# Loads, parameters and stores change queues in a batch-norm-and-ReLU kernel

## Chip, cores and metric

One core of one Trainium2 chip. The metric is device time in microseconds (us). The kernel before takes 83.91 us (median of 5 runs, 83.83 to 84.08). Its runs agree within 0.3%, so half a microsecond is a real difference here.

## The reference

```python
batch, channels, h, w = 32, 128, 32, 32        # x: 16.78 MB of float32
normalized = (x - running_mean[None,:,None,None]) / np.sqrt(running_var[None,:,None,None] + eps)
scaled = normalized * gamma[None,:,None,None] + beta[None,:,None,None]
return np.maximum(scaled, 0).astype(np.float32)
```

Each channel has one scale and one bias, so the kernel reads 16.78 MB, applies one activation `relu(scale*x + bias)`, and writes 16.78 MB.

## The kernel before

The 4096 rows of 1024 numbers (batch and channel together) are laid on 128 partitions, 16 consecutive rows to a partition, in two halves `t`. A half is cut into pieces by rows. Six loads (1, 1, 2, 4, 4 and 4 MiB) go out on the sync queue; four tiny parameter loads and all stores go out on the scalar queue, which is ScalarE's own.

```python
PIECES = (((0, 2), (2, 4), (4, 8), (8, 16)), ((0, 8), (8, 16)))
STORE_CUTS = {(0, 1)}
...
for t in range(T):
    for a, b in PIECES[t]:
        xt = data.tile([P, b - a, HW], F32, name=f"x{t}_{a}")
        nc.sync.dma_start(out=xt, in_=xr[t, :, a:b, :])
        tiles.append((t, a, b, xt))
raw = params.tile([Q, 4, J], F32, name="raw")
for k, src in enumerate((running_var, gamma, running_mean, beta)):
    nc.scalar.dma_start(out=raw[:, k, :], in_=src.rearrange("(q j) -> q j", j=J))
...   # a matmul spreads the parameters over the partitions; sqrt, reciprocal, products
for t, a, b, xt in tiles:
    first = a
    for j in range(a, b):
        nc.scalar.activation(out=xt[:, j-a, :], in_=xt[:, j-a, :], func=ACTF.Relu,
                             bias=bias_t[:, j:j+1], scale=scale_t[:, j:j+1])
        if j + 1 == b or (t, j + 1) in STORE_CUTS:
            nc.scalar.dma_start(out=outr[t, :, first:j+1, :], in_=xt[:, first-a:j+1-a, :])
            first = j + 1
```

## Time and profile before

| | before |
|---|---|
| time, median | 83.91 us |
| span of the profiled execution | 81.9 us |
| busiest compute engine (ScalarE) | 47% |
| bytes moved | 33.56 MB |
| mean rate over the span | 410 GB/s |

The prediction works out from the profile what bounds the kernel, and shows the lines that this rests on.

### The profile page before, as it was taken

What the parts mean: (1) busy time and instruction counts of PE and PEld (TensorE: products, weight loads), DVE (VectorE), ACT (ScalarE), POOL (GpSimd) and SP (SyncE); (2) the same over time, 40 slices, a digit from 0 to 9 for tenths busy, and PEclk for the clock granted to TensorE, in tenths of its full rate; (3) what the DMA queues carried; (4) which work ended last, traced back from release to release, by engine and by line L of the source; (5) the groups of instructions that cost most, each with busy time, mean ns of one, the idle gap of its engine ahead of it and who ended that gap; (6) DMA issues with size and microseconds to landing.
All of it is one profiled execution on the core that took longest, in us unless ns stands there. A gap on an engine that the chain in (4) does not pass through costs nothing.

```text
span 81.9 us, 119 instructions
## 1 busy us (share of the span) xinstructions
PE 0.7 (1%) x2; PEld 0.5 (1%) x2; DVE 0.8 (1%) x5; ACT 38.5 (47%) x34; POOL 0.8 (1%) x6
## 2 busy tenths in 40 slices
PE   0002000000000000000000000000000000000000
PEld 0002000000000000000000000000000000000000
DVE  0000300000000000000000000000000000000000
ACT  0600377799039999199994199993000000000000
POOL 3000000000000000000000000000000000000000
DMA  2899999989899999979789798996999899799690
GB/s 32 328 425 472 408 448 448 512 352 494 370 448 416 446 418 396 500 296 600 320 380 580 304 464 384 512 512 288 480 512 400 368 512 448 320 512 496 272 512 0
DMA packets 1936, 33.56 MB, mean 410 GB/s; under 512 B 272, under 2 KB 272, under 8 KB 528
## 3 DMA queue, kind: packets, MB, share of 16 engines
q1 hardware_dynamic: 864, 16.78, 48.4%
q10 hardware_dynamic: 1072, 16.78, 47.8%
HBM read 16.78 MB, written 16.78 MB: 410 GB/s over the span
## 4 chain that ended last, share of the span: by engine, by line
DMA 56%; ACT 11%; SPq 0%; issue 0%
DMA x<-in_x_dram 56%; ACT x L96 11%; SPq L52 0%
## 5 line engine op out<-in xcount | busy, mean ns | idle before, releaser
L96 ACT ACTIVATE x<-x,bias_t,scale_t 128x1024 f32<-128x1024 f32 x32 | 37.0, 1228 | 10.3 <-DMA x<-in_x_dram 7.9
L82 ACT ACT_TABLE_LOAD x1 | 1.3, 1283 | 2.6 <-issue 2.6
L82 ACT ACTIVATE std_t<-cols,eps_t 128x16 f32<-128x16 f32 x1 | 0.3, 273 | 4.5 <-PE cols L74 4.5
L74 PE MATMUL cols<-raw,rep 8*128 8x64 f32 x2 | 0.7, 428 | 7.7 <-DMA raw<-in_beta_dram 7.7
L74 PEld LDWEIGHTS cols<-raw,rep 8*128 8x128 f32 x2 | 0.5, 304 | 7.7 <-issue 7.7
L64 POOL TENSOR_SCALAR_AFFINE_SELECT rep<-rep 8x128 f32<-8x128 f32 x1 | 0.4, 392 | 0.1
L84 DVE RECIPROCAL rstd_t<-std_t 128x16 f32<-128x16 f32 x1 | 0.3, 254 | 7.8 <-ACT std_t L82 7.8
L63 POOL MEMSET rep<- 8x128 f32 x1 | 0.2, 195 | 0.3 <-POOLq L124 0.3
L86 DVE TENSOR_TENSOR scale_t<-cols,rstd_t 128x16 f32<-128x16 f32 x1 | 0.2, 175 | 0.1
L90 DVE TENSOR_TENSOR bias_t<-cols,ms_t 128x16 f32<-128x16 f32 x1 | 0.2, 175 | 0.0
L88 DVE TENSOR_TENSOR ms_t<-cols,scale_t 128x16 f32<-128x16 f32 x1 | 0.2, 175 | 0.0
L124 POOL MEMSET const-bfloat16-1.0<- 128x1 bf16 x1 | 0.1, 106 | 0.0
L124 POOL MEMSET const-uint8-127<- 128x1 uint8 x1 | 0.1, 106 | 0.0
L124 POOL MEMSET const-float32-0.0<- 128x1 f32 x1 | 0.1, 103 | 0.3 <-issue 0.3
L124 POOL MEMSET const-float32-1.0<- 128x1 f32 x1 | 0.1, 103 | 0.0
L61 DVE MEMSET eps_t<- 128x1 f32 x1 | 0.1, 59 | 0.9 <-PEq L124 0.9
## 6 DMA issues: line engine op xcount, KB each, us to landing
x<-in_x_dram SPq DMA_DIRECT2D x3, 4096.0 KB, 38.8
out_dram<-x ACTq DMA_DIRECT2D x3, 4096.0 KB, 27.9
x<-in_x_dram SPq DMA_DIRECT2D x2, 1024.0 KB, 5.7
x<-in_x_dram SPq DMA_DIRECT2D x1, 2048.0 KB, 11.2
out_dram<-x ACTq DMA_DIRECT2D x1, 2048.0 KB
out_dram<-x ACTq DMA_DIRECT2D x2, 512.0 KB, 18.8
out_dram<-x ACTq DMA_DIRECT2D x1, 1024.0 KB
raw<-in_running_var_dram ACTq DMA_DIRECT2D x1, 0.5 KB
```

The costliest lines, as they stand in the source:

```text
L61: nc.vector.memset(eps_t, float(eps))
L63: nc.gpsimd.memset(rep, 1.0)
L64: nc.gpsimd.affine_select(out=rep, in_=rep, compare_op=mybir.AluOpType.is_equal, fill=0.0, base=0, pattern=[[0, P // Q], [-1, Q]], channel ...
L74: nc.tensor.matmul(cols.rearrange("p k j -> p (k j)"), rep.rearrange("q r s -> q (r s)"), raw.rearrange("q k j -> q (k j)"), start=True, s ...
L82: nc.scalar.activation(out=std_t, in_=cols[:, 0, :], func=ACTF.Sqrt, bias=eps_t[:, 0:1], scale=1.0)
L84: nc.vector.reciprocal(out=rstd_t, in_=std_t)
L86: nc.vector.tensor_mul(out=scale_t, in0=cols[:, 1, :], in1=rstd_t)
L88: nc.vector.tensor_mul(out=ms_t, in0=cols[:, 2, :], in1=scale_t)
L90: nc.vector.tensor_sub(out=bias_t, in0=cols[:, 3, :], in1=ms_t)
L96: nc.scalar.activation(out=xt[:, j - a, :], in_=xt[:, j - a, :], func=ACTF.Relu, bias=bias_t[:, j : j + 1], scale=scale_t[:, j : j + 1],)
L124: nc = _bacc.Bacc("TRN2", target_bir_lowering=False, num_devices=1)
```

## The change

The intent: start the activations sooner, take store issues off ScalarE's queue, and save one store. The first load stays on the sync queue and goes out alone. The scalar queue issues the parameters first, then the other five loads, with a small square root between them that pulls the table load forward. All stores go to the sync queue. The fourth and fifth tiles are stored together.

```diff
-PIECES = (((0, 2), (2, 4), (4, 8), (8, 16)), ((0, 8), (8, 16)))
+TILES = (((0, 0, 2),), ((0, 2, 4),), ((0, 4, 8),), ((0, 8, 16), (1, 0, 8)), ((1, 8, 16),))
-            nc.sync.dma_start(out=xt, in_=xr[t, :, a:b, :])          # all six loads
-        nc.scalar.dma_start(out=raw[:, k, :], ...)                   # parameters
+        nc.sync.dma_start(out=loads[0][0], in_=loads[0][1])
+        for k, src in enumerate((running_var, gamma, running_mean, beta)):
+            nc.scalar.dma_start(out=raw[:, k, :], ...)
+        for i, (dst, src) in enumerate(loads[1:]):
+            nc.scalar.dma_start(out=dst, in_=src)
+            if i == 2:
+                nc.scalar.activation(out=first_t, in_=eps_t, func=ACTF.Sqrt)
 ...
-                    nc.scalar.dma_start(out=outr[t, :, first:j+1, :], ...)
+                        nc.sync.dma_start(out=outr[t, :, a+first:j+1, :], ...)
+            if len(pieces) == 2:      # both pieces of the double tile in one store
+                nc.sync.dma_start(out=bass.AP(tensor=outr.tensor, offset=...,
+                    ap=[[J*HW, P], [pitch, 2], [HW, b-a], [1, HW]]), in_=xt)
```

More of the change, by code (lines that the diff above doesn't have):

```diff
@@ L14 @@
 J = 16
-PIECES = (((0, 2), (2, 4), (4, 8), (8, 16)), ((0, 8), (8, 16)))
-STORE_CUTS = {(0, 1)}
+TILES = (((0, 0, 2),), ((0, 2, 4),), ((0, 4, 8),), ((0, 8, 16), (1, 0, 8)), ((1, 8, 16),))
+STORE_CUTS = {(0, 0)}
 @with_exitstack
@@ L48 @@
     tiles = []
-    for t in range(T):
-        for a, b in PIECES[t]:
-            xt = data.tile([P, b - a, HW], F32, name=f"x{t}_{a}")
-            nc.sync.dma_start(out=xt, in_=xr[t, :, a:b, :])
-            tiles.append((t, a, b, xt))
+    loads = []
+    for pieces in TILES:
+        n = len(pieces)
+        rows = pieces[0][2] - pieces[0][1]
+        xt = data.tile([P, n, rows, HW], F32, name=f"x{pieces[0][0]}_{pieces[0][1]}")
+        for i, (t, a, b) in enumerate(pieces):
+            loads.append((xt[:, i], xr[t, :, a:b, :]))
+        tiles.append((pieces, xt))
     raw = params.tile([Q, 4, J], F32, name="raw")
-    for k, src in enumerate((running_var, gamma, running_mean, beta)):
-        nc.scalar.dma_start(out=raw[:, k, :], in_=src.rearrange("(q j) -> q j", j=J))
     eps_t = params.tile([P, 1], F32, name="eps_t")
     nc.vector.memset(eps_t, float(eps))
+    first_t = params.tile([P, 1], F32, name="first_t")
+    with tc.manual_schedule(engines={mybir.EngineType.Activation, mybir.EngineType.SP}):
+        nc.sync.dma_start(out=loads[0][0], in_=loads[0][1])
+        for k, src in enumerate((running_var, gamma, running_mean, beta)):
+            nc.scalar.dma_start(out=raw[:, k, :], in_=src.rearrange("(q j) -> q j", j=J))
+        for i, (dst, src) in enumerate(loads[1:]):
+            nc.scalar.dma_start(out=dst, in_=src)
+            if i == 2:
+                nc.scalar.activation(out=first_t, in_=eps_t, func=ACTF.Sqrt)
     rep = params.tile([Q, P // Q, Q], F32, name="rep")
@@ L90 @@
     nc.vector.tensor_sub(out=bias_t, in0=cols[:, 3, :], in1=ms_t)
-    with tc.manual_schedule(engines={mybir.EngineType.Activation}):
-        for t, a, b, xt in tiles:
-            first = a
-            for j in range(a, b):
-                nc.scalar.activation(
-                    out=xt[:, j - a, :],
-                    in_=xt[:, j - a, :],
-                    func=ACTF.Relu,
-                    bias=bias_t[:, j : j + 1],
-                    scale=scale_t[:, j : j + 1],
-                )
-                if j + 1 == b or (t, j + 1) in STORE_CUTS:
-                    nc.scalar.dma_start(
-                        out=outr[t, :, first : j + 1, :], in_=xt[:, first - a : j + 1 - a, :]
-                    )
-                    first = j + 1
+    with tc.manual_schedule(engines={mybir.EngineType.Activation, mybir.EngineType.SP}):
+        for pieces, xt in tiles:
+            first = 0
+            for i, (t, a, b) in enumerate(pieces):
+                for j in range(a, b):
+                    nc.scalar.activation(
+                        out=xt[:, i, j - a, :],
+                        in_=xt[:, i, j - a, :],
+                        func=ACTF.Relu,
+                        bias=bias_t[:, j : j + 1],
+                        scale=scale_t[:, j : j + 1],
+                    )
+                    if len(pieces) == 1 and (j + 1 == b or (t, j) in STORE_CUTS):
+                        nc.sync.dma_start(
+                            out=outr[t, :, a + first : j + 1, :], in_=xt[:, 0, first : j + 1 - a, :]
+                        )
+                        first = j + 1 - a
+            if len(pieces) == 2:
+                (t0, a, b), (t1, c, _) = pieces
+                pitch = ((t1 - t0) * P * J + c - a) * HW
+                nc.sync.dma_start(
+                    out=bass.AP(
+                        tensor=outr.tensor,
+                        offset=outr[t0, :, a:b, :].offset,
+                        ap=[[J * HW, P], [pitch, 2], [HW, b - a], [1, HW]],
+                    ),
+                    in_=xt,
+                )
 _INS = ['x', 'gamma', 'beta', 'running_mean', 'running_var', 'eps']
```

## The prediction

> **What bounds the kernel now.** I read the page first, then the load by stage, then the timeline with the waits, to see whether any wait reaches the end. The page:
>
> ```profile
> span 81.9 us, 119 instructions
> PE 0.7 (1%) x2; PEld 0.5 (1%) x2; DVE 0.8 (1%) x5; ACT 38.5 (47%) x34; POOL 0.8 (1%) x6
> DMA  2899999989899999979789798996999899799690
> HBM read 16.78 MB, written 16.78 MB: 410 GB/s over the span
> DMA 56%; ACT 11%; SPq 0%; issue 0%
> ```
>
> No compute engine is busy for more than 47% of the span, and the DMA row is 7 to 9 in all slices but the first and the last. 33.56 MB must pass. The chain (the last line) is no guide here: it names the wait for the last load and then eight activations, but shows nothing of the store traffic after that. So I took the rate in the stages (columns: stretch, length, busy time of each engine with its count, clock, DMA share, GB/s):
>
> ```profile
> 0.00:2.00 2.00, 0.00 (x0) 0.00 (x0) 0.06 (x1) 0.00 (x0) 0.80 (x6) 1.00 0.20 29
> 2.00:4.00 2.00, 0.00 (x0) 0.00 (x0) 0.00 (x0) 1.28 (x1) 0.00 (x0) 1.00 0.85 324
> 4.00:14.00 10.00, 0.65 (x2) 0.49 (x2) 0.78 (x4) 3.64 (x4) 0.00 (x0) 1.00 1.07 454
> 14.00:46.00 32.00, 0.00 (x0) 0.00 (x0) 0.00 (x0) 24.43 (x22) 0.00 (x0) 1.00 0.99 422
> 46.00:80.00 34.00, 0.00 (x0) 0.00 (x0) 0.00 (x0) 9.16 (x8) 0.00 (x0) 1.00 1.01 436
> 80.00:82.00 2.00, 0.00 (x0) 0.00 (x0) 0.00 (x0) 0.00 (x0) 0.00 (x0) 1.00 0.00 0
> ```
>
> From 4 us to 80 us the 16 DMA engines are full (share 0.99 to 1.07, so a little over one packet in flight each) in all stages: loads alone, loads beside stores, stores alone. 33.56 MB at the 436 GB/s of the pure store stage is 77.0 us. The span is 81.9, so only 4.9 us are not this transfer: some 2 before the first packet, about half a microsecond of slow start (324 GB/s between 2 and 4), 1.3 to 1.9 after the last packet, and around a microsecond lost between.
>
> What counts next is how much stored data is queued when the loads run out. In the stretch from 14 to 46 us the two queues moved (packets, MB, share of 16 engines):
>
> ```profile
> q1 hardware_dynamic: 384, 11.53, 83.9%
> q10 hardware_dynamic: 399, 1.96, 14.7%
> ```
>
> q1 is the load queue, q10 the store queue. They sent nearly equally many packets, but loads have 32 KB in each (eight rows per partition) and the first stores 4 KB (one row). So the stores hardly move until the loads are over at about 46 us, and pile up. The timeline says when work was handed over:
>
> ```profile
> 8.42 0.27 ACT L82 ACTIVATE std_t<-cols,eps_t 128x16 f32<-128x16 f32 x1 [4.52 <-PE cols L74]
> 9.72 1.24 ACT L96 ACTIVATE x<-x,bias_t,scale_t 128x1024 f32<-128x1024 f32 x1 [1.03 <-DVE bias_t L90]
> 23.86 9.16 ACT L96 ACTIVATE x<-x,bias_t,scale_t 128x1024 f32<-128x1024 f32 x8 [3.32 <-DMA x<-in_x_dram]
> 33.05 0.34 ACTq L104 DMA_DIRECT2D out_dram<-x  x1
> 34.81 9.16 ACT L96 ACTIVATE x<-x,bias_t,scale_t 128x1024 f32<-128x1024 f32 x8 [1.79 <-DMA x<-in_x_dram]
> 44.00 0.34 ACTq L104 DMA_DIRECT2D out_dram<-x  x1
> 46.79 9.16 ACT L96 ACTIVATE x<-x,bias_t,scale_t 128x1024 f32<-128x1024 f32 x8 [2.82 <-DMA x<-in_x_dram]
> 55.97 0.34 ACTq L104 DMA_DIRECT2D out_dram<-x  x1
> ```
>
> Four stores with 0.5+0.5+1+2 = 4 MiB (4.19 MB) precede the three large ones. By 46 us only 1.96 MB of them have gone; the rest, 2.23 MB, needs 2.23/0.436 = 5.1 us, to about 51. So the first large store, issued at 33.05, has nothing to do for 18 us, and the last, issued at 55.97, isn't reached before 51 + 2 x 4.19/0.436 = 70.5. ScalarE has some 15 us to spare at the end.
>
> **What the skill says.** The Trainium skill, "DMA: Bandwidth & Descriptors", section "Issuing engines are not separate DMA queues", says that transfers from sync and scalar run on the same 16 engines and that a second issuing engine saves only sequencer time. The trace agrees: share about 1.0 whether one queue works or two. Its section "Queues, rings and completion order" says that each engine alternates between queues packet by packet; 384 against 399 packets agrees. "Where 436 GB/s comes from" puts the ceiling of the 16 ports at 435 GB/s; the store stage shows 436, so nothing is left there for a queue arrangement. "ScalarE: Activation LUTs", "What ACT_TABLE_LOAD costs", has a load at about 1283 ns; the trace shows 1.28 us, between 2.6 and 3.9, beside idle waiting.
>
> **The change, part by part.**
>
> *First load alone on the sync queue.* It is still issued at 0.81, as the first instruction of that queue. Zero change of the start of the stream. The second load now comes from the scalar queue behind four parameter issues (0.59, 0.29, 0.31 and 0.45 us in the timeline, done at 2.53), so at 2.6 instead of 1.2. The first load's 1.05 MB needs 2.4 us at 436 GB/s, and with the slow start it drains at about 5. The second load's issue at 2.6 plus one microsecond from issue to first packets (0.81 to about 1.8 for the first) is 3.6: in time. I allow 0 to 0.4 us for an engine that changes queue[...].
>
> *Parameters.* Their tiny packets alternated with two loads' packets of q1, and the last landed at about 7.6. Now only the first load stands against them, and what is left follows when it drains: landing at about 5.5. Matmul to first main activation took 9.72 - 7.73 = 2.0 us, so the activations can start at about 7.6 instead of 9.7: 2 us earlier.
>
> *Five loads and the table load on ScalarE.* Three loads at 0.40 us median end at about 3.8, table load and the new small square root 1.6 more (5.4), two loads 0.7 (6.1). That ends before the 6.3 at which the matmul result is there. Costs nothing. The trace has eight semaphores for all transfers, reused in order of issue (in before, a load sat 4.1 us for a parameter's landing). The fifth and sixth load are ninth and tenth transfer; they would wait for the first load or the first parameter, landing by about 5.3, so the table load fills just that time.
>
> *Stores on the sync queue.* Seven issues of 0.34 to 0.38 us, 2.4 us in sum, leave ScalarE; three of them (0.42 to 0.46 us gaps) stood between activations with data present. With the earlier start ScalarE then waits for loads instead, as it already does for the fourth to sixth tile (3.3, 1.8 and 2.8 us). Nothing reaches the end. A store becomes available some 2 to 3 us sooner, so perhaps two or three more small packets per engine go between loads: loads end some 0.5 to 1 us later (at 47), and exactly as much less store traffic is left.
>
> *Merged store.* The fourth and fifth tiles leave together as 8.39 MB when the fifth is done. It landed at 34.8; I take 35.5, plus 9.2 us, so issue at about 44.7 in place of 33.05 and 44.00. The four stores ahead of it last to about 51. Slack 6 us, against some 1 us from issue to first packets. One store's completion entries saved: under 0.1 us. The packets stay 32 KB (two runs of eight rows per partition).
>
> Sum: 81.9 + 0 (start) + 0.1 (queue change, middle of 0 to 0.4, less what is saved) + 0 (rate, bytes unchanged) + 0 (tail, the last store is again queued 14 us early) = 82.0, and the unprofiled time is about what it was, 83.9.
>
> **The rivals.** (1) *The merged store runs the DMA dry.* If the early stores drained well before 44.7, engines would idle until it arrives. For it: the first of its halves is held back by 11 us. Against it: 1.96 MB in 32 us beside loads. Only a share of half the bytes for stores would empty the queue by 30; then loads alone fill the engines to about 50 anyway, and the gap would be 1 to 1.5 us: 85 to 85.5. (2) *The sooner start gains.* The intent of the change: activations 2 us earlier, no store issues on ScalarE. If ScalarE were on the path the gain would be 2 to 3 us: 81.5. The chain's 11% for ScalarE speaks for it, the full DMA row from 46 to 80 against it. (3) *A load on ScalarE's queue waits for a semaphore of a late transfer,* holding activations back. Eight semaphores and ten early transfers make it possible. Even 5 us later the store queue would still fill before the loads end: 83.9. Only a late last store (waiting for the merged one to land) would open a gap of 1.5 to 2 us: 85.7. (4) *Mixed stage runs better or worse.* At 422 instead of 436 GB/s it costs 32 x 14/436 = 1.0 us; other packet pairs might win or lose a third of that: 83.6 to 84.2.
>
> **Range and chances.** The centre is the sum. The lower end takes rival 4's gain with some of that microsecond lost, 83.3; the upper the whole 0.4 at the start and a little of a gap, 84.6. Faster than 82.3 would need 1.6 of the 4.9 us that aren't transfer: 3%. Slower than 85.6 needs rival 1 or 3 in full: 4%.
>
> **What would show it right or wrong.** Right: first packets at about 1.8 us and the last at about 80.5; share near 1.0 from 4 to 80; first main activation at 7 to 8.5; merged store issued at 43 to 46, and store traffic unbroken around 51. Wrong if a slice in the middle drops below the rate, if the stretch from 4 to 6 shows a hole where the second load should follow, if the early stores have moved far more than 2 MB by the time the loads end with the merged store yet to come, or if sync waits for a landing before the last store.

## The result, and the profile after

| | before | after |
|---|---|---|
| time, median of 5 | 83.91 us | 85.42 us (85.31 to 85.68) |
| span of the profiled execution | 81.9 us | 83.7 us |
| ratio | | 1.0179, 95% interval 1.0160 to 1.0198 |

A ratio here is the mean time of one kernel's fast runs over that of the other's of the same rounds, so it is not quite the ratio of the medians. The change is 1.5 us slower: not slower than 85.6, for which the prediction had given 4%, but above its range of 83.3 to 84.6.

The page after (span; busy DMA in 40 slices; rate in the slices):

```profile
span 83.7 us, 120 instructions
DMA  1999998989897989897999899979998999999760
GB/s 43 372 365 434 462 477 356 509 337 524 342 503 337 509 356 487 354 552 337 407 509 356 348 423 509 470 313 485 454 454 360 485 454 391 407 501 454 329 266 0
```

There is no hole. But where the DMA row before ended in 6, 9, 0, with 272, 512 and 0 GB/s, it now tapers: 7, 6, 0, with 329, 266 and 0 GB/s. The timeline of the start after (start, length, engine, line, operation; the letter q after an engine's name marks its issuing queue):

```profile
0.81 0.38 SPq L68 DMA_DIRECT2D x<-in_x_dram  x1
2.07 0.32 ACTq L70 DMA_DIRECT2D raw<-in_beta_dram  x1
2.41 1.32 ACTq L72 DMA_DIRECT2D x<-in_x_dram  x3
...
6.51 0.27 ACT L96 ACTIVATE std_t<-cols,eps_t 128x16 f32<-128x16 f32 x1 [1.25 <-PE cols L88]
7.81 3.51 ACT L111 ACTIVATE x<-x,bias_t,scale_t 128x1024 f32<-128x1024 f32 x3 [1.03 <-DVE bias_t L104]
9.08 0.34 SPq L119 DMA_DIRECT2D out_dram<-x  x1
```

The compute side did what was intended: first main activation at 7.81 (9.72 before), first store at 9.08 (10.99 before). The second load goes out at 2.41, where the trace of before has it at 1.23. Later in the same timeline:

```profile
36.53 9.17 ACT L111 ACTIVATE x<-x,bias_t,scale_t 128x1024 f32<-128x1024 f32 x8 [2.09 <-DMA x<-in_x_dram]
45.72 0.38 SPq L127 DMA_DIRECT2D out_dram<-x  x1
50.27 9.17 ACT L111 ACTIVATE x<-x,bias_t,scale_t 128x1024 f32<-128x1024 f32 x8 [4.57 <-DMA x<-in_x_dram]
59.46 0.34 SPq L119 DMA_DIRECT2D out_dram<-x  x1
```

The merged store goes out at 45.72, well before the store queue reaches it at about 52. The same stretches of both kernels (last columns: clock, DMA share, GB/s), first before:

```profile
4.00:6.00 2.00, 0.00 (x0) 0.00 (x0) 0.00 (x0) 0.00 (x0) 0.00 (x0) 1.00 1.01 418
40.00:48.00 8.00, 0.00 (x0) 0.00 (x0) 0.00 (x0) 5.18 (x6) 0.00 (x0) 1.00 1.03 443
81.00:83.00 2.00, 0.00 (x0) 0.00 (x0) 0.00 (x0) 0.00 (x0) 0.00 (x0) 1.00 0.00 0
```

and after:

```profile
4.00:6.00 2.00, 0.18 (x1) 0.21 (x2) 0.00 (x0) 1.25 (x2) 0.00 (x0) 1.00 1.01 374
40.00:48.00 8.00, 0.00 (x0) 0.00 (x0) 0.00 (x0) 5.70 (x6) 0.00 (x0) 1.00 1.00 404
81.00:83.00 2.00, 0.00 (x0) 0.00 (x0) 0.00 (x0) 0.00 (x0) 0.00 (x0) 1.00 0.04 16
```

Two stretches carry fewer bytes (374 against 418, 404 against 443) although the share says "busy" in both. A packet counts as busy while it is under way, so a packet that takes longer looks like work. Here the share hides the loss and the GB/s column shows it. (The view counts a packet whole in the stretch in which it begins, so figures of short stretches are coarse.)

The third pair is the tail. Each full transfer ends in sixteen completion entries of a few bytes, one for each DMA engine. Of the last store, all sixteen fall between 80 and 81 us before. After, the DMA view of the stretches 80 to 81, 81 to 82 and 82 to 83 has:

```profile
DMA packets 16, 0.16 MB, mean 164 GB/s; under 512 B 11, under 2 KB 11, under 8 KB 11
...
DMA packets 5, 0.03 MB, mean 33 GB/s; under 512 B 4, under 2 KB 4, under 8 KB 4
...
DMA packets 1, 0.00 MB, mean 0 GB/s; under 512 B 1, under 2 KB 1, under 8 KB 1
```

Eleven engines are done in the first of these microseconds, four in the second, and one holds up the kernel until 82.9. Nothing evens this out: in the last three stores the slowest landing is 1.82, 1.79 and 1.80 us behind the first (at 53.88, 73.23 and 82.91 us), and the next slowest 1.24, 1.21 and 1.22. It is as if each engine had a fixed part of every transfer; the trace does not name the engines. The completion times in the trace show where it began (first, median and last of the sixteen engines):

| landing of | before | after |
|---|---|---|
| first load | 5.18, 5.33, 5.49 | 4.88, 5.11, 5.43 |
| second load | 7.68, 7.84, 7.97 | 7.53, 7.77, **8.87** |
| third load | 12.58, 12.74, 12.88 | 12.54, 12.70, **14.26** |
| last load | 46.40, 46.56, 46.76 | 47.17, 47.40, **50.25** |
| last store | 80.67, 80.75, 80.97 | 81.11, 81.30, **82.91** |

So the 1.94 us by which the last landing is later (80.97 to 82.91) is two things. **Stragglers:** the slowest engine is 1.61 us behind the median instead of 0.22, which is 1.39 us. They arise at the second load and have not caught up at the end (the wider gap at the last load, 2.85 us, closes again to about 1.6). **A common loss:** the median itself is 0.55 us later. Most of it is lost near the end of the loads: a 32 KB load packet takes 1.213 us as a rule, but the last ones, between 44 and 48 us, took 0.3 to 1.0 us longer, 7.2 us in sum, or 0.45 us for each of 16 engines. The kernel before has no such packet there.

Not all of the 1.94 us reaches the time. From the last landing to the end of the span it takes 0.93 us before and 0.83 after; the same 0.83 stands in every other kernel with six stores, and 0.93 again in those with seven (e2, e4, e11), so this 0.10 seems to be what one store fewer saves (e9, with five stores and one load fewer, has 0.95, so it is no plain count). The time is longer than the span by 1.88 us before, and by 1.69 to 1.74 in the changed kernel and all sixteen variants (means over the runs; why is not known), which is another 0.16. 1.94 less these is the 1.68 between the two profiled executions (83.77 and 85.45); the medians lie 1.51 apart.

### The profile page after: what moved, and what is told of

The parts are those of the page before. It is cut to its first block, busy times and chain, and to the rows that moved or that the text cites. A ratio compares the mean times of both kernels' runs of the same rounds, so it can differ in the third digit from the quotient of the medians.

```text
span 83.7 us, 120 instructions
## 1 busy us (share of the span) xinstructions
PE 0.7 (1%) x2; PEld 0.5 (1%) x2; DVE 0.8 (1%) x5; ACT 38.5 (46%) x35; POOL 0.8 (1%) x6
## 4 chain that ended last, share of the span: by engine, by line
DMA 59%; ACT 10%; ACTq 1%; issue 0%
DMA x<-in_x_dram 59%; ACT x L111 10%; ACTq L165 1%
```

## The experiments

Sixteen kernels ran; all gave the right result. Each time is a median of 5 or 6 runs, and the kernel before ran beside them at 83.81, 83.85, 83.86 and 83.86 in the four sets of four. "Spread" is last minus first landing of the last store (before 0.29, after 1.80); "slow packets" is the sum of the extra time of 32 KB load packets that began between 41 and 48 us.

| kernel | second load issued | first store issued | time | ratio | spread | slow packets |
|---|---|---|---|---|---|---|
| e1 | 0.81 | 15.89 | 84.18 | 1.0041 | 0.37 | 9.9 |
| e2 | 2.40 | 9.52 | 85.40 | 1.0178 | 2.05 | 6.9 |
| e3 | 1.21 | 10.59 | 83.64 | 0.9978 | 0.40 | 0.0 |
| e4 | 2.65 | 9.52 | 85.27 | 1.0156 | 1.56 | 1.5 |
| e5 | 0.81 | 12.54 | 84.02 | 1.0023 | 0.35 | 1.2 |
| e6 | 3.13 | 9.57 | 84.06 to 84.22, see text | 1.0033 | 0.43 | 10.3 |
| e7 | 0.81 | 16.87 | 84.26 | 1.0045 | 0.49 | 11.3 |
| e8 | 1.21 | 17.18 | 84.26 | 1.0045 | 0.52 | 13.3 |
| e9 | 2.46 | 11.74 | 84.05 | 1.0022 | 0.33 | 0.4 |
| e10 | 2.24 | 9.71 | 85.31 | 1.0158 | 0.81 | 0.1 |
| e11 | 1.21 | 10.56 | 83.74 | 0.9989 | 0.49 | 0.0 |
| e12 | 1.21 | 14.25 | 84.20 | 1.0036 | 0.46 | 7.6 |
| e13 | 1.41 | 10.44 | 83.57 | 0.9960 | 0.36 | 1.2 |
| e14 | 1.21 | 14.24 | 84.62 | 1.0083 | 0.42 | 9.6 |
| e15 | 1.24 | 10.94 | 83.60 | 0.9966 | 0.41 | 0.2 |
| e16 | 1.20 | 10.52 | 83.62 | 0.9964 | 0.33 | 0.1 |

The spreads and slow packets come from one profiled execution of each kernel, the times from all. The runs of most kernels lie within 0.6 us; e2, e4 and e10 scatter by 1.0 us (84.84 to 85.84, 84.46 to 85.47, 84.50 to 85.53), e6 by 2.0. Diffs are against the changed kernel unless another is named.

### First set: where do the stragglers come from?

My first theory (A): the parameters now stand right ahead of the second load in its own queue, and as they touch only 8 of the 16 engines (eight packets of 64 bytes for each parameter in the trace), they put those behind. Its first rival (B): the changeover from one queue to the other costs. The other theory of this set, M, is that handing over the merged store causes the slow packets.

**e1: parameters to the sync queue.**

```diff
-            nc.scalar.dma_start(out=raw[:, k, :], ...)
+            nc.sync.dma_start(out=raw[:, k, :], ...)
```

> The changed kernel, with the four parameter loads moved from the head of the scalar queue to the sync queue, behind the first load; the scalar queue carries loads alone. Theory A (the parameters stand in the same queue right ahead of the second load, on 8 of the 16 DMA engines, and put those engines behind): the landing of the second load is no longer spread (all 16 engines within 0.4 us instead of 1.3), the last store's too, and the time falls by about 1.4 us to 84.0. Theory B (the changeover from the sync queue to the scalar queue itself is what costs): nothing gained, 85.2 to 85.6, and the last store lands over 1.5 us or more.

84.18 us, the second load's landing within 0.33 us, stragglers gone. B has fallen: the load stream is still split between the queues. But not all came back; the slow packets are still there, at 42 to 45 us.

**e2: merged store undone.**

```diff
-... ((0, 8, 16), (1, 0, 8)), ((1, 8, 16),))
+... ((0, 8, 16),), ((1, 0, 8),), ((1, 8, 16),))
```

> The changed kernel with the merged store undone: six single tiles, each stored when it is done, seven stores. Theory M (handing over the merged store stops all engines for about 0.4 us: the load packets under way at 45 to 47 us took 0.3 to 0.6 us longer than the others): those long packets are gone and the time falls by 0.4 to 0.5 us to about 85.0. Rival (the stop belongs to the end of the loads, whichever store is issued): long packets remain near 45 us and the time stays at 85.4. The spread of the last landing, 1.8 us, stays in either case.

85.40 us, slow packets as in the changed kernel (6.9 against 7.2). The times alone are unclear, as two of the six runs are at M's 85.0 or just below (84.84, 84.92); by the packets M has fallen. Merging makes no difference of note to the time.

**e3: all loads on scalar, parameters and stores on sync.**

```diff
-        nc.sync.dma_start(out=loads[0][0], in_=loads[0][1])
+        nc.scalar.dma_start(out=loads[0][0], in_=loads[0][1])
-            nc.scalar.dma_start(out=raw[:, k, :], ...)
+            nc.sync.dma_start(out=raw[:, k, :], ...)
```

> The changed kernel with all six loads on the scalar queue and the four parameter loads on the sync queue: no changeover between queues within the load stream, and no parameters ahead of a load in its queue. Theories A and B both expect the spread gone and about 84.0. If the spread of 1.3 us in the second load's landing stays, the cause is neither, but that loads go out on the scalar queue at all (theory C): about 85.4.

83.64 us: no stragglers, no slow packets, a little below the kernel before, and below the 84.0 that A and B expected. So the scalar queue carries loads as well as the sync queue does.

**e4: the kernel before, with the parameters between its first and second load.**

```diff
 # against the kernel before (cut: the loop stands in a manual schedule of the sync queue)
                 nc.sync.dma_start(out=xt, in_=xr[t, :, a:b, :])
+                if not tiles:
+                    for k, src in enumerate((running_var, gamma, running_mean, beta)):
+                        nc.sync.dma_start(out=raw[:, k, :], ...)
-    nc.scalar.dma_start(out=raw[:, k, :], ...)
```

> The kernel before, with its four parameter loads on the sync queue between the first and the second load; all loads and parameters in one queue, stores on the scalar queue. Theory A: the eight engines that carry parameters fall behind here as well, landing of the second load spread over 1 us, time 85 to 85.4. Theories B and C: no spread, 83.8 to 84.1.

85.27 us (spread 1.56): the stragglers are reproduced in the kernel before, without a change of queue. That looked like proof of A. But these four kernels share something else: in e4 and e2 the second load is issued at 2.4 to 2.65, because four issues of about 0.3 us stand ahead of it; in e1 and e3 it is issued at 0.81 and 1.21. A and the issue time had moved together. I had to make theory D out of this: not the parameters, but the late issue.

### Second set: A against D, and two theories of the slow packets

For the slow packets: S1, the first load in the stores' queue does it (e1 has it, e3 does not); S2, the time at which the stores start does it.

**e5: second load ahead of the parameters.**

```diff
+        nc.scalar.dma_start(out=loads[1][0], in_=loads[1][1])
         for k, src in enumerate((running_var, gamma, running_mean, beta)):
             nc.scalar.dma_start(out=raw[:, k, :], ...)
-        for i, (dst, src) in enumerate(loads[1:]):
+        for i, (dst, src) in enumerate(loads[2:]):
...
-            if i == 2:
+            if i == 1:          # the small square root stays behind the fourth load
```

> The changed kernel with one move: the second load goes ahead of the four parameters on the scalar queue (first load still alone on sync, then stores there). Theory A (parameter packets right ahead of a load in its queue put some DMA engines behind): the spread moves to the third load, over 1 us, and the time stays at 85 or more. Theory D (not the parameters but the late issue of the second load, 2.4 us instead of 1.2[...]): second load issued at 0.8, all landings within 0.5 us of each other, time 84.0 to 84.3, what then remains over 83.8 being the slow load packets near the end of the loads, as in e1.

84.02 us, no stragglers at the end (the third load landed over 0.69 us, the next over 0.48). As D expects, but for that 0.69, a little over its 0.5; parameters right ahead of the third load do little.

**e6: e3 with the second load held back.**

```diff
 # against e3
+    nc.vector.memset(tiles[1][1], 0.0)
```

> The all-loads-on-scalar kernel (e3, 83.64) with the second load held back by a memset of its tile on VectorE, no parameter in its queue. If the memset holds it to 2.4 us or later, theory D expects a spread of 1 us or more in the second load's landing that stays to the last store, and 84.6 to 85.4; theory A expects no spread and 83.6 to 83.8. If the memset is too short to hold it past 1.8, nothing is told.

The load went out at 3.13. Three executions took 84.06 to 84.22, three 85.39 to 86.09; the latter are marked slow because they are over 1.5% above the fastest, and the profile is of a quick one, with no straggler. The kernel before, in the same rounds, had no such execution. I take nothing from the slow-marked runs: inconclusive. D had expected 84.6 to 85.4 and a spread of 1 us or more, and the three quick executions don't show it; but the clock is 1.00 in all six, so the mark rests on the time alone and may have sorted out just the executions with stragglers. No profile of one is kept.

**e7: e1 with the queues exchanged.**

```diff
 # against e1: every dma_start on nc.sync goes to nc.scalar, and the reverse
```

> e1 with the two queues exchanged: first load, parameters and stores on scalar, the other five loads on sync. If the remaining loss of e1 (load packets 0.3 to 0.5 us slower near the end of the loads, 0.6 us in sum) comes from the first load sharing the stores' queue (S1) or from late stores (S2), it is here too: 84.1 to 84.4. If it comes from which of the two queues carries the loads, it is gone: 83.6 to 83.9.

84.26 us, slow packets 11.3. Which engine's queue carries what does not matter.

**e8: e3 with the parameters behind the third load.**

```diff
 # against e3
-        for k, src in ...: nc.sync.dma_start(out=raw[:, k, :], ...)
         for i, (dst, src) in enumerate(loads[1:]):
             nc.scalar.dma_start(out=dst, in_=src)
+            if i == 1:
+                for k, p_src in ...: nc.scalar.dma_start(out=raw[:, k, :], ...)
```

> e3 with the four parameter loads moved onto the scalar queue between the third and the fourth load: they land at about 13 us, activations start at about 15 as in e1, but the first load isn't in the stores' queue. S1 (first load in the stores' queue is what costs the 0.6 us near the end of the loads): no slow packets, 83.6 to 83.9. S2 (the later start of the stores shifts what stands beside the last loads): slow packets, 84.1 to 84.4. Theory A expects a spread of 1 us from the fourth load on and over 85; theory D none.

84.26 us, slow packets 13.3 with the first load not in the stores' queue: S1 has fallen. There are parameters in the load queue, and no stragglers: against A.

### Third set: the decision

**e9: a first load of 2 MiB.**

```diff
-TILES = (((0, 0, 2),), ((0, 2, 4),), ((0, 4, 8),), ...
+TILES = (((0, 0, 4),), ((0, 4, 8),), ...
```

> The changed kernel with a first load of 2 MB instead of 1 (four rows; the second 1 MB load is gone, stores cut accordingly). The parameters still stand at the head of the scalar queue and the next load is still issued at 2.4, but now the first load keeps the engines busy to 7.3 instead of 4.9. Theory D (late issue relative to the end of the first load): landings of all loads within 0.5 us, last store's too, time 83.8 to 84.5. Theory A (parameter packets ahead of a load in its queue): spread over 1 us in the second load's landing and at the end, 85 or more.

84.05 us, spread 0.33. The parameters stand ahead of the next load and it is issued at 2.46 (2.41 in the changed kernel); what differs is that the first load lasts longer, and with it that there is one load and one store fewer. A has fallen. (The first load itself landed over 1.4 us here, while the next load was already under way in the other queue; that one landed within 0.36.) The slow packets are not absent, as the table suggests: sixteen began between 25.7 and 26.0 us, outside its stretch.

**e10: e6 with a shorter memset.**

```diff
 # against e6
-    nc.vector.memset(tiles[1][1], 0.0)
+    nc.vector.memset(tiles[1][1][:, :, :, 0:600], 0.0)
```

> e6 with a shorter memset, so that the second load is issued at about 2.4 as in the changed kernel, but with no parameters in its queue. Theory D: engines fall behind in most executions, 84.8 to 85.6 in those. Theory A: none, 83.6 to 84.3 in all. If some do and some do not, as in e6, lateness alone is a risk and the parameters ahead make it regular.

85.31 us, six runs (five between 85.14 and 85.53, one 84.50, which is the profiled one). The load queue holds no parameters, and the second load goes out at 2.24. The stretches of e10:

```profile
4.00:6.00 2.00, 0.01 (x1) 0.04 (x1) 0.00 (x0) 1.06 (x2) 0.00 (x0) 1.00 1.02 320
40.00:48.00 8.00, 0.00 (x0) 0.00 (x0) 0.00 (x0) 5.41 (x5) 0.00 (x0) 1.00 0.96 413
```

and of e3:

```profile
4.00:6.00 2.00, 0.00 (x0) 0.00 (x0) 0.00 (x0) 0.32 (x2) 0.00 (x0) 1.00 1.02 427
40.00:48.00 8.00, 0.00 (x0) 0.00 (x0) 0.00 (x0) 5.14 (x5) 0.00 (x0) 1.00 1.03 441
```

320 GB/s where the first load gives way to the second, against 427 in e3 and 374 in the changed kernel. What was altered against e3 (83.64) is the issue time of the second load and of those behind it; the memset that does this also writes to the tile, but e13's and e6's do so too, and neither has stragglers. D stands, with e6 as its exception: all 23 executions with a first load of 1 MiB and the second issued at 2.24 to 2.65 us (changed kernel, e2, e4, e10) took 84.46 or more and 20 of them 84.9 or more, those issued by 1.41 at most 84.71 (e14); but e6's quick three, issued at 3.13, took 84.06 to 84.22.

**e11: e3 with the merged store undone.** The edit is that of e2.

> e3 (all loads on scalar, parameters and stores on sync) with the merged store undone. If the merged store is neutral, as e2 says, 83.5 to 83.8, and no slow load packets at the end of the loads; if merging itself gained, 83.8 to 84.1.

83.74 us. Against e3 the merged store is worth 0.1 us, about the 0.10 seen after the last landing. (The profiled execution, 84.10, was the slowest of the six; it had slow packets around 35.7 us. The other five, at 83.67 to 83.78, have no profile.)

**e12: e3 with later stores.**

```diff
 # against e3, ahead of the reciprocal
+    for _ in range(5):
+        nc.vector.memset(idle_t, 0.0)      # [128, 2048]
```

> e3 with the activations held back by about 1.5 us through memsets on VectorE ahead of the scale's reciprocal; loads and queues as in e3. S2 (the moment at which the stores start sets whether the last load packets run slow): first store issued at 12 instead of 10.6, slow load packets between 42 and 46, 83.9 to 84.4. If the slow packets come from anything else that e1 and e5 to e8 have in common, none here: 83.5 to 83.8.

84.20 us in all runs (84.09 to 84.29), first store at 14.25 (I had expected 12), slow packets 7.6:

```profile
40.00:48.00 8.00, 0.00 (x0) 0.00 (x0) 0.00 (x0) 4.99 (x6) 0.00 (x0) 1.00 0.97 391
```

e3 has 441 GB/s in the same stretch. Only the time of activations and stores was moved against it (and VectorE kept busy until then). S2 holds so far: a later start brings the slow packets here.

### Fourth set: how late, which neighbour, and the mended kernel

**e13: e10 with a shorter memset still.**

```diff
 # against e10
-    nc.vector.memset(tiles[1][1][:, :, :, 0:600], 0.0)
+    nc.vector.memset(tiles[1][1][:, :, :, 0:200], 0.0)
```

> e10 with a shorter memset still: second load issued at about 1.75 instead of 2.24 (e10, 85.31) and 1.21 (e3, 83.64), no parameters in its queue. Theory D[...]: nothing lost yet, 83.6 to 84.3. Theory D without slack (every delay costs): 84.3 to 85, spread of 0.5 to 1 us.

The issue came at 1.41, not 1.75, so this tells less than planned: 83.57 us, 0.2 us later than in e3 costs nothing. The limit for a first load of 1 MiB lies between 1.41 and 2.24.

**e14: e12 with single rows stored.**

```diff
 # against e12
-STORE_CUTS = {(0, 0)}
+STORE_CUTS = {(0, j) for j in range(8)}
```

> e12 with each of the first eight rows stored by itself, so that all store packets beside the last loads are 4 KB instead of 8. If 8 KB store packets beside them are what slows the last load packets, no slow packets from 42 to 46 and 83.6 to 83.9; if it is the moment in the load stream and not the neighbour, slow packets stay and 84.1 to 84.4.

84.62 us, above both expected ranges; slow packets 9.6 beside 4 KB stores. The size of the neighbouring packets is not the cause. (Of the 0.42 us over e12, 0.26 lie after the last landing, 1.09 against 0.83, with ten stores for six.)

**e15: the changed kernel with one load moved.**

```diff
         nc.sync.dma_start(out=loads[0][0], in_=loads[0][1])
+        nc.sync.dma_start(out=loads[1][0], in_=loads[1][1])
         for k, src in ...: nc.scalar.dma_start(out=raw[:, k, :], ...)
-        for i, (dst, src) in enumerate(loads[1:]):
+        for i, (dst, src) in enumerate(loads[2:]):
...
-            if i == 2:
+            if i == 1:          # the small square root stays behind the fourth load
```

> The changed kernel with the second load on the sync queue behind the first (issued at 1.2), parameters and the other four loads on scalar as in the change. Theory D: no spread over 0.6 us at the second or the last landing, 83.7 to 84.3, the remainder being slow packets near the end of the loads if they are there. If queue roles matter otherwise: 85 or more.

83.60 us, ratio 0.9966 (0.9951 to 0.9981). One moved load takes back the whole loss, 1.8 us against the changed kernel. My expectation of a small spread at the second landing was wrong (7.76 to 10.27; the other queue's loads are under way beside it), but by the third load all engines are together (12.40 to 12.72), and at the end:

```profile
40.00:48.00 8.00, 0.00 (x0) 0.00 (x0) 0.00 (x0) 5.15 (x5) 0.00 (x0) 1.00 1.00 427
48.00:79.00 31.00, 0.00 (x0) 0.00 (x0) 0.00 (x0) 8.02 (x8) 0.00 (x0) 1.00 1.00 431
79.00:81.00 2.00, 0.00 (x0) 0.00 (x0) 0.00 (x0) 0.00 (x0) 0.00 (x0) 1.00 0.61 262
81.00:83.00 2.00, 0.00 (x0) 0.00 (x0) 0.00 (x0) 0.00 (x0) 0.00 (x0) 1.00 0.00 0
```

No tail after 81. The parameters still head the scalar queue, and the other roles are those of the change.

**e16: e3 again.** No edit.

> e3 again, unchanged, as it is the only version below the kernel before: 83.5 to 83.8 if the gain of 0.2 us is real, 83.8 to 84.0 if it was chance.

83.62 us, ratio 0.9964 (0.9949 to 0.9978). With e3's first 0.9978, the 0.2 to 0.3 us below the kernel before is real. But it isn't the transfers that are faster: the last landing is at 81.06 (e3), 80.95 (e16) and 81.02 (e15), where the kernel before has 80.97. The gain is the 0.10 us after it and the 0.16 outside the span that the changed kernel has too. e3 and e15 are the versions to keep; they cannot be told apart.

## Why the prediction was wrong

*The bound* was right: DMA, in every stage. The main activations on ScalarE began 1.9 us earlier and it brought nothing, as the prediction said against rival 2.

*The step that failed* is "First load alone on the sync queue". It had the facts: second load issued at about 2.6 (measured 2.41), first packets possible one microsecond later, engines working on the first load until 5. It concluded "in time", and put 0 to 0.4 us on the changeover, 0.1 in the sum; no line of a trace stood behind the 0.4. That term measured 1.39 us of stragglers at the last landing. Two things were wrong with it. It took the moment at which the engines finish the first load as the deadline; the runs show an earlier one, between 1.41 and 2.24 us as issue time for a first load of 1 MiB (e13, e10), and none reached at 2.46 with 2 MiB (e9). And it reckoned with the mean engine, where the end is set by the slowest: the median landing of the second load is not late at all in the changed kernel (7.77 against 7.84), only the later ones of the sixteen are (up to 8.87). Nor is it the change of queue that costs, as the term had it: e4 and e10 keep all loads in one queue and lose, e15 changes queue and doesn't.

Why the deadline is that early is not shown. The trace shows in what form the time is lost: not as idle engines (counting only the part of each packet inside the stretch, they are busy 0.99 of the time from 4 to 6 us after, and 0.99 in e10) but as slower packets. The 8 KB load packets that began between 4.5 and 7 us took 0.31 us on average before and in e3, 0.35 after, and 0.40 in e10, with single ones up to 1.48. And e6, issued later still, has no stragglers in its profile, which a deadline alone doesn't explain. That stays open.

*The rate term* was put at 0. It measured 0.45 us in the last load packets. I had allowed for a changed mix (rival 4, up to 0.3 us), so the kind was foreseen and the size was not. In e12 against e3 it came with a later start of activations and stores; it doesn't come from the merged store (e2), which queue carries what (e7), the first load's queue (e8) or the neighbours' packet size (e14). In e3, e11, e13, e15, e16 and in the kernel before, whose first stores go out at 10.4 to 11.0, it is 0 to 1.2 us in sum; in seven others 7 to 13. But the changed kernel itself starts its stores earlier, at 9.08, and has 7.2; e10, with 9.71, has 0.1, e4, with 9.52, has 1.5, and e5, with 12.54, has 1.2, so the start of the stores is not the whole of it. Nor is the end of the loads: the slow packets come mostly in one or two bursts of 11 to 17, each within a microsecond, and while most bursts lie between 41 and 46 us, e9 has its at 25.8 and e11 at 35.7. The mechanism is open.

*Right in their mechanism:* parameters by 5.7 (said 5.5); main activations at 7.81 (7.6); merged store at 45.72 (44.7, with slack left); 1.92 MB stored between 14 and 46 us against 1.96 before, so the store queue never ran dry; last store 12 us before its queue reached it (said 14; the sum behind it is 51 + 19.2 = 70.2, not 70.5). With one store fewer, 0.10 us less follow the last landing (said under 0.1). Rivals 1 and 3 cost nothing. Not foreseen were the 0.16 us outside the span; the prediction took that part as unchanged.

*Of the stated signs,* "the stretch from 4 to 6 shows a hole where the second load should follow" came true, as 374 for 418 GB/s and not as an empty slice. So did the drop in the middle (332 for 426 GB/s from 44 to 48), and the last packet, between 82 and 83 us, missed the 80.5 of the right signs. "Share near 1.0 from 4 to 80" held and told nothing.

## What to carry to other kernels

At the start of a stream of transfers, issue the second one right behind the first, or beside it in another queue, ahead of everything small; here it wasn't enough that it could start before the first one ended. In a kernel bound by DMA, look at the last landing of each transfer, not at the mean share: here the slowest was 1.1 us behind the median at the second load and still 1.6 behind at the last store. One wide landing alone is no such lag (e15's second load landed over 2.5 us, its third over 0.3); see whether the later ones are wide too. And check two experiments that agree for a second thing that both have changed; here the issue time hid behind the parameters until a memset moved it alone.

## What the Trainium skill lacked or had wrong

- "DMA: Bandwidth & Descriptors", section "Issuing engines are not separate DMA queues": it says a further issuing engine saves only issue time, usually small beside the transfer. True of the rate here, but issue time can cost more than itself: 1.2 us of later issue (2.41 for 1.23) with work still on the engines became 1.4 us at the end, and 1.0 us of it (e10 against e3) made 1.7 us between the medians.
- The same page, section "Queues, rings and completion order": it tells that engines alternate packet by packet, not that the bytes are then shared by packet size. From 14 to 46 us of the kernel before, 384 packets carried 11.53 MB of loads and 399 packets 1.96 MB of stores.
- No page says that a lag of the slowest engine is carried on through all later transfers to the end of the program; here 1.1 us behind the median at the second load, 1.6 at the last store 74 us later.
- "Perfetto Trace Analysis", section "Identifying the Most-Contended Engine", warns that occupancy of 16 DMA engines misleads; the runs show how: share 1.01 in both kernels from 4 to 6 us, at 418 and 374 GB/s.
